# Two small-tile groups padded and moved, so that large SBUF tiles start at multiples of 128 bytes

## The chip, the cores and the metric

The kernel runs as one program on one core of a Trainium2 chip. What counts is the device time of one execution in microseconds (us). Before the change the median of 3 runs is 2946.0 us (2944.36 to 2950.4). "Product" below means one TensorE matrix product: a weight load (LDWEIGHTS) of a stationary operand of 128 x 128 values, and a MATMUL that streams a moving operand of 256 or 512 columns past it.

## What is computed

The reference runs two blocks on one sequence of 512 tokens with 1,024 channels, all in float32.

The first block has two layers. A layer is a SwiGLU feed-forward part of width 2,816 (`x + 0.5 * rms_norm(swiglu(rms_norm(x))))`), a token-mixing part (sliding-window attention with rotary positions, an mLSTM and an RWKV-7 recurrence, joined and projected), a second feed-forward part, and a gated per-layer embedding. The second block is an attention block (global grouped-query attention and a dilated-window mixture) and a feed-forward part with a 3-tap convolution over tokens and a GELU gate.

```python
def first_block(x, ...):
    for l in range(DEPTH):                       # 2 layers
        x = x + 0.5 * rms_norm(swiglu(rms_norm(x, ...), w_ffn1_in[l], w_ffn1_out[l]), ...)
        x = x + rms_norm(token_mixing(rms_norm(x, ...), ...), ...)
        x = x + 0.5 * rms_norm(swiglu(rms_norm(x, ...), w_ffn2_in[l], w_ffn2_out[l]), ...)
        gate = sigmoid(rms_norm(x, ...) @ w_ple_gate[l])
        x = x + rms_norm(gate * (p[l] @ w_ple_proj[l]), ...)
def second_block(x, ...):                        # after it
    x = x + mixed @ w_out                        # two attentions
    x = x + conv_ffn(rms_norm_2(x, norm2_g), w_up, conv_w, conv_b, w_down)
```

## The kernel before

**Precision.** Every large product is done with three products of rounded halves (`mm3`, L284 to L289): an operand is split into a rounded part and a rest (`xh` and `xl`, `wh` and `wl`, the two halves of `ts`, of `gs`, of `wx`), ScalarE making the rounded part (L275, L435) and VectorE the rest (L276, L437). L287 multiplies rounded by rounded, L288 and L289 rounded by rest. The 4-byte values stay in SBUF; TensorE reads both operands from there.

**Stages.** `run` calls, for each layer, `ffn` (L634), `mix` (L758), `ffn` again and `ple`, with `rope_tables` once after the first `ffn`, and at the end `block2`, whose last part is a feed-forward phase called `ffn2`. Within a feed-forward part, the input products go in pairs of 128-channel tiles. The first `FIRST` = 2 pairs are classical products (names `psmm<-...`). The others go through `fast_pair` (L450), which replaces eight products of halves by seven (names `psfast<-...`): for each pair 7 x 4 x 3 = 84 products of 256 moving columns. Of the seven, numbers 0, 1 and 5 stream parts of `xh` and `xl`; 2, 3 and 4 stream the sums `ts`; number 6 streams `xh` and `xl` in the four `ffn` calls and a further pair of `ts` tiles in `ffn2` (`keep=True`). The output products (`ffn_out`, `proj_n8`) have tokens on partitions: `gs` is stationary, and weight tiles `wh` and `wl`, in the last group of four `wx`, stream with 512 columns (names `psone<-...`). `mix` uses `psmm` and `pspn` products for its projections, and small products for its recurrences; `block2` uses `pspn` and `psone` products and small ones for its attentions.

**Order.** The order of the instructions on each engine is the order of the program text; `weave` and `staggered` interleave generators by fixed rates. SyncE's queue starts the weight loads (`raw`, 512 KB each, three buffers), GpSimd's queue the gains.

**Where tiles lie.** Tiles stand in pools, and in each partition a pool's tiles follow one another, each rounded up to 32 bytes. Pools follow one another in the order of `setup`: `const` (with `x`, `ct`, `xh`, `xl`, `mhalf`, and the tables `cos` and `sin` that `rope_tables` adds), `wr` (`raw`), `ws` (`wh`, `wl`), `t4`, `t2` and `sg`, and above them the pools of the running phase: first `sm_...` with the small tiles, then the phase's own, such as `g` (11 tiles), `wx` and `yb` in the same places, and `T0` to `T5` (`ts`, later `gs`). `x` starts at a multiple of 128 bytes. `ct` holds 2,402 values, 9,608 bytes, which take 9,632. So `xh` and `xl` (16,384 bytes each) start 32 bytes past a multiple of 128; `mhalf`, `cos` and `sin` take 320 bytes, and `wr`, `ws` and `t4` start 96 past one. The 28 small tiles of `sg` take 896 bytes, so the tiles of the `ffn` phases start 96 past too. In `ffn2` a tile `cv` of 704 bytes comes first, and `g` and `T0` to `T7` start 32 past.

Of the kernel before, what the change touches and what calls it, by code (L numbers as in the profile page):

```python
# [9 lines left out]
F32 = mybir.dt.float32  # L10
# [9 lines left out]
NT, P = 4, 128  # L20
# [5 lines left out]
# ------------------------------------------------------------------ constants (shapes alone)  # L26


def _const_table():
    """Name -> [128, n] tables that depend on the shapes alone."""  # L30
# [55 lines left out]
# per-channel vectors of a layer, [128, n] columns  # L86
PV_OFF, PV_N = _offsets({k: np.zeros((1, n)) for k, n in (
    ("mu", 8), ("w0", 2), ("a0", 2), ("kk", 2), ("ka", 2), ("rk", 2), ("conv", 16))})
# per-token rows of a layer
# [7 lines left out]
def lay_out(inp):  # L97
    """The inputs in the layouts that the kernel loads: reshapes, transposes, slices and joins."""
# [4 lines left out]
    def chans(v):  # [n*128] -> [128, n]  # L103
        return v.reshape(-1, P).T
# [10 lines left out]
    def t_chunks(w):  # [K, n*128] -> [n, 128, 8, 128]  # L115
        return c(w.reshape(KD, P, -1, P).transpose(2, 1, 0, 3))

    def n_chunks(w):  # [K, n] -> [128, K/128, n]
        return c(w.reshape(-1, P, w.shape[1]).transpose(1, 0, 2))

    def halves(w):  # [K, 1024] -> [2, 128, K/128, 512]
        return c(w.reshape(-1, P, 2, 512).transpose(2, 1, 0, 3))
# [30 lines left out]
def staggered(gens, depth, lag):  # L153
    """The generators one after another, up to depth of them at a time, each lag steps behind the one before."""
    todo, live = list(gens), []
    since = lag
    while todo or live:
        if todo and len(live) < depth and (since >= lag or not live):
            live.append(todo.pop(0))
            since = 0  # L160
        for g in list(live):
            if next(g, live) is live:
                live.remove(g)
        since += 1
        yield


def weave(*streams):
    """Advance the generators together, each by its number of steps in turn (a fraction: now and then)."""
    live = [[g, rate, 0.0] for g, rate in streams]  # L170
    while live:
        for s in list(live):
            s[2] += s[1]
            while s[2] >= 1:
                s[2] -= 1
                if next(s[0], live) is live:
                    live.remove(s)
                    break


# products between the steps of a stream, and rates of the streams woven together
LAG, EARLY, OTHERS, DELTA, SLIDING, MLSTM = 24, 1, 2, 1, 1.3, 1
FIRST = 2  # pairs of tiles by classical products; the rest by fast_pair


class Kernel:
    def __init__(self, tc, io, out):
        self.tc, self.nc, self.io, self.out = tc, tc.nc, io, out
        self.order = list("ABCD")  # pairs of banks, those that are free first first
# [4 lines left out]
    # -------------------------------------------------------------- pools and constants  # L194
    def setup(self, es):
# [10 lines left out]
        self.ct = self.const.tile([P, C_N], F32, name="consts")  # L206

        def early_x(t):
# [5 lines left out]
                     lambda: nc.sync.dma_start(self.ct[:, P:], self.io["consts"][:, P:])]  # L214
# [3 lines left out]
        nc.gpsimd.memset(self.mhalf, -0.5)  # L218

# [14 lines left out]
    def ring(self, **rings):  # L234
        """Name the pairs of banks that bank() takes in turn."""
# [28 lines left out]
    # -------------------------------------------------------------- pieces  # L264
    def rsqrt(self, out, in_, scale, add, tag="rs"):
        """out = (in_ * scale + add) ** -0.5"""
# [6 lines left out]
    def split(self, h, l, src):  # L273
        """h + l = src exactly; each has 12 significant bits."""
# [9 lines left out]
    def mm3(self, out, a, b, start, stop, **kw):  # L284
        """out += a[0+1]^T b[0+1]"""
# [5 lines left out]
    def norm_begin(self):  # L291
        """Begin on the next of the norms; its tokens may come while the phase before still ends."""
# [15 lines left out]
    def norm_token(self):  # L308
        """rms_norm(x) * gain of the next 128 tokens, transposed and split"""
# [23 lines left out]
    def norm_t(self):  # L333
        """The next norm's result, transposed and split: two tiles [128, 8, 512]"""
# [7 lines left out]
    def norm_fast(self):  # L342
        """norm_t, with what fast_parts takes"""
# [29 lines left out]
    def fast_parts(self, pool, ps, keep=False):  # L373
        """What the products of fast_pair take: B[k half][token half] = [[b11, b12], [b21, b22]] gives t1 = b12 - b11,
        t2 = b22 - t1, t3 = b22 - b12 and t4 = b21 - t2"""
# [25 lines left out]
    def ahead(self, jobs):  # L401
        """jobs are (what prepares, what takes that and returns what is left to do); each is prepared before the one
        before it does what is left"""
# [17 lines left out]
    def fast_weights(self, w1, w2):  # L421
        """What fast_pair takes of w1 = [a11 a12] and w2 = [a21 a22], chunks [128, 8, 128]: a11, a12, s2, s1, s3, s4
        and a22, with s1 = a21 + a22, s2 = s1 - a11, s3 = a11 - a21, s4 = a12 - s2, each split"""
# [26 lines left out]
    def fast_pair(self, ws, xb, top, low):  # L450
        """[top; low] = [a11 a12; a21 a22]^T B in seven products of halves (Strassen, Winograd's form); the low half's
        first tokens stay in PSUM."""
# [31 lines left out]
    def proj_t_steps(self, xs, tiles, first=0):  # L484
        """Transposed products: tiles is a list of (chunk [128, 8, 128] in DRAM, what takes the sum).
        The first ones go by token halves, as the later tokens come later."""
# [25 lines left out]
    def proj_n_steps(self, lhs, jobs, ahead=1):  # L512
        """Products with tokens on partitions: lhs(k, t) -> (hi, lo) [128, 128]; the jobs are (w [128, 8, n] in
        DRAM, what takes (token tile, sum), its ring of banks); the pieces of w come some pairs of k ahead."""
# [25 lines left out]
    def proj_n8(self, lhs, w, kn, take, pairs, pool=None, last=4, group=3, ahead=True):  # L540
        """Products with tokens on partitions, up to 1024 columns at once: w [128, kn, n] in DRAM, pairs the
        banks of the tokens, pool(i) two tiles for the pieces of the last group, or None; take(t, sums). With
        ahead the next norm begins before the end."""
# [41 lines left out]
    def post8(self, gain, mul, room):  # L585
        """What takes y [512, 1024]: x += mul * rms_norm(y) * gain; room(t) is a tile [128, 2, 512] for y * gain"""
# [20 lines left out]
    # -------------------------------------------------------------- ffn  # L607
# [62 lines left out]
    # -------------------------------------------------------------- per-layer embedding  # L670
# [38 lines left out]
    # -------------------------------------------------------------- rope tables of the first block  # L709
    def rope_tables(self):  # L710
        self.load_late()
        self.cos = self.const.tile([P, NT, 8], F32, name="cos")
        self.sin = self.const.tile([P, NT, 8], F32, name="sin")
# [3 lines left out]
    def rope_tables_(self):  # L717
        """cos and sin of positions * inv_freq, [128, 4, 8]; the angles are reduced to [-pi, pi] for any
        int32 position: first by multiples of 2 pi 2^11, then of 2 pi, each constant in short parts whose
        products with the counts are exact."""  # L720
# [36 lines left out]
    # -------------------------------------------------------------- token mixing  # L757
    def mix(self, l):  # L758
# [3 lines left out]
        with self.phase(f"mix{l}") as pool:  # L762
            tl = lambda name, shape, dt=F32: pool.tile(list(shape), dt, tag=name, name=name)
            pv = tl("pv", [P, PV_N])
            nc.sync.dma_start(pv, io[f"pv{l}"])
            rows = tl("rows", [P, RW_N])
            nc.gpsimd.dma_start(rows, io[f"rw{l}"][0].partition_broadcast(P))
# [10 lines left out]
            omu = tl("omu", [P, 8])  # L778
            V.tensor_scalar(omu, pv[:, PV_OFF["mu"][0]:PV_OFF["mu"][0] + 8], -1.0, 1.0, ALU.mult, ALU.add)
            hb = tl("hb", [P, 4])  # L780
            V.tensor_scalar(hb, pv[:, PV_OFF["w0"][0]:PV_OFF["w0"][0] + 4], 0.5, None, ALU.mult)
            oka = tl("oka", [P, 2])
# [6 lines left out]
            # ---- rwkv: products, token shift  # L789
# [37 lines left out]
            def prepare():  # L827
# [7 lines left out]
                for i in range(2):  # L835
# [21 lines left out]
                    # kk, normalised by head  # L857
# [34 lines left out]
            # ---- rwkv: blocks of 128 tokens, chunks of 64  # L892
# [4 lines left out]
            def group(t):  # L897
# [9 lines left out]
                # heads of one parity share the rows of the array, and have banks of their own  # L907
# [126 lines left out]
                # group norm, bonus, gate  # L1034
# [24 lines left out]
            # ---- the other products  # L1059
# [35 lines left out]
            def others():  # L1095
# [5 lines left out]
                while len(ab) < 2:  # its tiles are prepare's before  # L1101
                    yield
# [8 lines left out]
            # ---- the three together  # L1111
# [6 lines left out]
            # ---- out  # L1118
# [18 lines left out]
    def sliding(self, pool, qk, va, sinks, out):  # L1137
# [3 lines left out]
        for t in range(NT):  # L1141
            # rope
# [11 lines left out]
            # split, scaled by 1/8 for q, and transposed  # L1154
# [88 lines left out]
    def mlstm(self, pool, X, conv, vo, iff, row, out):  # L1243
# [3 lines left out]
        # gates, tokens on partitions  # L1247
# [7 lines left out]
        # log sigmoid(f) = -log(1 + e), e = exp(-f); log(1 + e) = e * log(w) / (w - 1), w = fl(1 + e)  # L1255
# [8 lines left out]
        # heads on partitions: G = cumsum(log f), a = i - G, M = cummax(a)  # L1264
# [71 lines left out]
    # -------------------------------------------------------------- second block  # L1336
    def block2(self):
# [3 lines left out]
        with self.phase("b2") as pool:  # L1341
# [18 lines left out]
            def head_stat(x, n):  # L1360
                """per-head rms norm of x [128, n, 64]: the scales"""
# [7 lines left out]
            def head_scale(x, r, gi, n):  # L1369
                """per-head rms norm of x [128, n, 64], in place"""  # L1370
# [23 lines left out]
            def head_norms(todo, depth=2):  # L1394
                """per-head norms in place, each after the scales of the next ones: todo is (x [128, n, 64], index of
                the gain, n, tokens for rope or None)"""
# [28 lines left out]
            # products of two 64-vectors a and b in two passes: [ah; al] with [bh; bl] and with [bl; bh]  # L1425
            def split_q(q, n):
                """Four heads, scaled by 1/8: [qh | ql]"""
# [9 lines left out]
            def split_k(src, dst):  # L1437
                """[kh | kl | kh]"""
# [24 lines left out]
            def prepare(kind, h):  # L1463
                """What head h of the first (kind 0) or second attention needs"""
# [92 lines left out]
            # norms of the outputs, transposed  # L1557
# [19 lines left out]
        with self.phase("ffn2") as pool:  # L1577
            cv = pool.tile([P, 4, 44], F32, name="cv")
            nc.sync.dma_start(cv, io["cv2"].rearrange("p (j m) -> p j m", j=4))
# [81 lines left out]
```

## Time and profile before

| what | before |
|---|---|
| median of 3 runs | 2946.0 us (2944.36 to 2950.4) |
| span of the profiled execution | 2960.7 us |
| TensorE matmuls | busy 2898.4 us (98%), 19,000 |
| TensorE weight loads | busy 2538.6 us (86%) |
| VectorE | busy 1953.1 us (66%) |
| ScalarE | busy 1425.6 us (48%) |
| GpSimd | busy 140.3 us (5%) |
| DMA | 250.91 MB, mean 85 GB/s |

The profile is of one execution, whose own time is its span; it stands 14.7 us (0.5%) above the median of the runs. "Busy" of a matmul runs from its start to a modelled end, and consecutive matmuls overlap, so the time that a product costs is read from start to start and not from its mean duration. The rows are quoted in the section ahead of the prediction.

### The profile page before, as it was taken

What the parts mean: (1) busy time and instruction counts of PE and PEld (TensorE: products, weight loads), DVE (VectorE), ACT (ScalarE), POOL (GpSimd) and SP (SyncE); (2) the same over time, 40 slices, a digit from 0 to 9 for tenths busy, and PEclk for the clock granted to TensorE, in tenths of its full rate; (3) what the DMA queues carried; (4) which work ended last, traced back from release to release, by engine and by line L of the source; (5) the groups of instructions that cost most, each with busy time, mean ns of one, the idle gap of its engine ahead of it and who ended that gap; (6) DMA issues with size and microseconds to landing.
All of it is one profiled execution on the core that took longest, in us unless ns stands there. A gap on an engine that the chain in (4) does not pass through costs nothing. (4 is left out here: it accounts for less than half of the span.)

```text
span 2960.7 us, 47335 instructions
## 1 busy us (share of the span) xinstructions
PE 2898.4 (98%) x19000; PEld 2538.6 (86%) x19000; DVE 1953.1 (66%) x3464; ACT 1425.6 (48%) x2784; POOL 140.3 (5%) x169
## 2 busy tenths in 40 slices
PE   7999999999999999999999999999999999999999
PEld 7998887877999878999887877799987877789987
DVE  7884555756888357886345655688635766688853
ACT  5663343343666245555334233456534456566641
POOL 0000000101000000000000000100000220000000
PEclk9999999999999999999999988999999999999999
DMA  4333322002233332333412000233343210313332
GB/s 152 108 122 103 97 81 65 8 8 65 93 115 115 100 103 90 109 107 116 130 56 79 15 8 29 75 107 111 114 128 90 93 43 1 93 62 104 100 101 91
DMA packets 74156, 250.91 MB, mean 85 GB/s; under 512 B 8112, under 2 KB 10416, under 8 KB 73680
## 3 DMA queue, kind: packets, MB, share of 16 engines
q1 hardware_dynamic: 70992, 236.99, 25.2%
q0 software_dynamic: 2944, 10.90, 1.1%
q8 instruction: 149, 2.44, 0.3%
q14 instruction: 71, 0.58, 0.1%
HBM read 245.76 MB, written 2.10 MB: 84 GB/s over the span
## 5 line engine op out<-in xcount | busy, mean ns | idle before, releaser
L276 DVE TENSOR_TENSOR wl<-raw,wh 128x1024 fp32r<-128x1024 f32 (+2 forms) x218 | 259.2, 1193 | 410.1 <-ACT wh L275 408.5
L275 ACT CAST wh<-raw 128x1024 fp32r<-128x1024 f32 (+2 forms) x218 | 223.4, 1026 | 469.9 <-PE psone L289 316.9
L287 PE MATMUL psfast<-xh,wh 128*128 128x256 f32 x1448 | 401.9, 278 | 0.0
L289 PE MATMUL psfast<-xh,wl 128*128 128x256 f32 x1448 | 400.7, 277 | 0.0
L288 PE MATMUL psfast<-xl,wh 128*128 128x256 f32 x1448 | 400.6, 277 | 0.0
L287 PE MATMUL psfast<-ts,wh 128*128 128x256 f32 x1184 | 333.1, 282 | 0.0
L289 PE MATMUL psfast<-ts,wl 128*128 128x256 f32 x1184 | 333.0, 281 | 0.0
L288 PE MATMUL psfast<-ts,wh 128*128 128x256 f32 x1184 | 332.5, 281 | 0.0
L288 PE MATMUL psone<-wl,gs 128*128 128x512 f32 x720 | 284.2, 395 | 0.0
L289 PE MATMUL psone<-wh,gs 128*128 128x512 f32 x720 | 284.1, 395 | 0.0
L287 PE MATMUL psone<-wh,gs 128*128 128x512 f32 x720 | 282.3, 395 | 0.0
L287 PEld LDWEIGHTS psfast<-xh,wh 128*128 128x128 f32 x1448 | 272.0, 188 | 1.3
L288 PEld LDWEIGHTS psfast<-xl,wh 128*128 128x128 f32 x1448 | 272.1, 188 | 0.5
L289 PEld LDWEIGHTS psfast<-xh,wl 128*128 128x128 f32 x1448 | 272.0, 188 | 0.0
L435 ACT CAST wh<-raw 128x512 fp32r<-128x512 f32 x282 | 174.7, 621 | 157.8 <-PE psfast L288 154.2
L287 PEld LDWEIGHTS psfast<-ts,wh 128*128 128x128 f32 x1184 | 222.7, 188 | 0.7 <-ACT top L465 0.7
L289 PEld LDWEIGHTS psfast<-ts,wl 128*128 128x128 f32 x1184 | 222.9, 188 | 0.0
L288 PEld LDWEIGHTS psfast<-ts,wh 128*128 128x128 f32 x1184 | 222.8, 188 | 0.0
L437 DVE TENSOR_TENSOR wl<-raw,wh 128x1024 fp32r<-128x1024 f32 (+1 forms) x188 | 179.1, 953 | 64.9 <-ACT wh L435 64.5
L287 PE MATMUL psmm<-xh,wh 128*128 128x256 f32 (+1 forms) x616 | 206.8, 338 | 0.1
L288 PE MATMUL psmm<-xl,wh 128*128 128x256 f32 (+1 forms) x616 | 205.8, 335 | 0.0
L289 PE MATMUL psmm<-xh,wl 128*128 128x256 f32 (+1 forms) x616 | 204.3, 333 | 0.0
(545 smaller groups left out, 6494.1 us busy)
## 6 DMA issues: line engine op xcount, KB each, us to landing
raw<-f1i SPq DMA_DIRECT2D x88, 512.0 KB, 3.5
raw<-f2i SPq DMA_DIRECT2D x88, 512.0 KB, 3.5
raw<-f1o SPq DMA_DIRECT2D x44, 512.0 KB, 3.7
raw<-f2o SPq DMA_DIRECT2D x44, 512.0 KB, 3.9
raw<-w2u SPq DMA_DIRECT2D x44, 512.0 KB, 3.5
raw<-w2d SPq DMA_DIRECT2D x22, 512.0 KB, 3.9
gain<-gains POOLq DMA_DIRECT2D x19, 512.0 KB, 4.0
raw<-wr SPq DMA_DIRECT2D x16, 512.0 KB, 3.6
```

The lines of the kernel that those rows point to most:

```text
L275: self.rounded = self.nc.scalar.copy(h, src)
L276: self.nc.vector.tensor_sub(l, src, h.bitcast(F32))
L287: mm(out, a[0], b[0], start=start, stop=False, **kw)
L288: mm(out, a[0], b[1], start=False, stop=False, **kw)
L289: mm(out, a[1], b[0], start=False, stop=stop, **kw)
L435: nc.scalar.copy(h[:, i], src[:, i])
L437: sub(l, src, h.bitcast(F32))
```

## The change

Small tiles get more room, and small tiles that stood alone share one:

- `ct` is allocated with 2,432 columns in place of 2,402 (9,728 bytes, 76 x 128).
- `cos` and `sin`, 128 bytes each and allocated in `rope_tables`, become two parts of one tile `tables` of 80 columns (320 bytes) in `setup`; with `mhalf` (64 bytes) that is 384 bytes, 3 x 128.
- In `mix`, `pv` has 64 columns in place of 34, `rows` 800 in place of 784; `omu`, `hb` and `oka`, three tiles before, become parts of one tile `vecs` of 32 columns.
- In `ffn2`, `cv` is [128, 4, 48] in place of [128, 4, 44], and its load fills the first 44 of each 48.

No operation of a compute engine is added or removed, and no loop changes. The loads of `ct`, `pv`, `rows` and `cv` bring the same bytes; that of `cv` writes four runs of 176 bytes in each partition where it wrote one of 704. The comments and doc strings of the file are removed too.

The positions that follow, as bytes past a multiple of 256 (and of 128 in brackets):

| tiles | before | after |
|---|---|---|
| `xh`, `xl` | 32 (32) | 128 (0) |
| `raw`, `wh`, `wl`, tiles of `t4` | 96 (96) | 0 (0) |
| `g`, `wx`, `ts`, `gs` in the four `ffn` | 224 (96) | 128 (0) |
| `g`, `wx`, `ts`, `gs` in `ffn2` | 160 (32) | 128 (0) |
| `x`, `ct` and its identity | 128 (0) | 128 (0) |

Within all these tiles the parts that TensorE reads begin at further multiples of 512 bytes, so a product's operands have the position of their tile. Of the large tiles only `vo1` to `vo3` in `mix` stay 32, 64 and 96 bytes past.

```diff
+LINE = 32
 FIRST = 2
@@ setup
-        self.ct = self.const.tile([P, C_N], F32, name="consts")
+        whole = lambda n: -(-n // LINE) * LINE
+        self.ct = self.const.tile([P, whole(C_N)], F32, name="consts")
...
-                     lambda: nc.sync.dma_start(self.ct[:, P:], self.io["consts"][:, P:])]
+                     lambda: nc.sync.dma_start(self.ct[:, P:C_N], self.io["consts"][:, P:])]
...
         nc.gpsimd.memset(self.mhalf, -0.5)
+        tables = self.const.tile([P, 3 * LINE - 16], F32, name="tables")
+        self.cos, self.sin = [tables[:, 32 * i:32 * i + 32].rearrange("p (t j) -> p t j", t=NT) for i in range(2)]
@@ rope_tables
-        self.cos = self.const.tile([P, NT, 8], F32, name="cos")
-        self.sin = self.const.tile([P, NT, 8], F32, name="sin")
@@ mix
-            pv = tl("pv", [P, PV_N])
-            nc.sync.dma_start(pv, io[f"pv{l}"])
-            rows = tl("rows", [P, RW_N])
-            nc.gpsimd.dma_start(rows, io[f"rw{l}"][0].partition_broadcast(P))
+            pv = tl("pv", [P, 2 * LINE])
+            nc.sync.dma_start(pv[:, 0:PV_N], io[f"pv{l}"])
+            rows = tl("rows", [P, 25 * LINE])
+            nc.gpsimd.dma_start(rows[:, 0:RW_N], io[f"rw{l}"][0].partition_broadcast(P))
...
-            omu = tl("omu", [P, 8])
+            vecs = tl("vecs", [P, LINE])
+            omu, hb, oka = vecs[:, 0:8], vecs[:, 8:12], vecs[:, 16:18]
             V.tensor_scalar(omu, pv[:, PV_OFF["mu"][0]:PV_OFF["mu"][0] + 8], -1.0, 1.0, ALU.mult, ALU.add)
-            hb = tl("hb", [P, 4])
             V.tensor_scalar(hb, pv[:, PV_OFF["w0"][0]:PV_OFF["w0"][0] + 4], 0.5, None, ALU.mult)
-            oka = tl("oka", [P, 2])
@@ block2, ffn2
-            cv = pool.tile([P, 4, 44], F32, name="cv")
-            nc.sync.dma_start(cv, io["cv2"].rearrange("p (j m) -> p j m", j=4))
+            cv = pool.tile([P, 4, 48], F32, name="cv")
+            nc.sync.dma_start(cv[:, :, 0:44], io["cv2"].rearrange("p (j m) -> p j m", j=4))
```

## Rows read from the trace of the kernel before

**Rows 1.** The page, part 1: busy time, share of the span, instructions of each engine.

```profile
PE 2898.4 (98%) x19000; PEld 2538.6 (86%) x19000; DVE 1953.1 (66%) x3464; ACT 1425.6 (48%) x2784; POOL 140.3 (5%) x169
```

**Rows 2.** The chain that ended last, shares of the span by engine.

```profile
PE 44%; DVE 2%; POOL 1%; ACT 1%; issue 0%; DMA 0%; POOLq 0%; ACTq 0%; DVEq 0%
```

**Rows 3.** Matmuls by form: line, out<-in, shapes, count | busy us, mean ns.

```profile
L287 PE MATMUL psfast<-xh,wh 128*128 128x256 f32 x1448 | 401.9, 278 | 0.0
L287 PE MATMUL psfast<-ts,wh 128*128 128x256 f32 x1184 | 333.1, 282 | 0.0
L287 PE MATMUL psone<-wh,gs 128*128 128x512 f32 x720 | 282.3, 395 | 0.0
L287 PE MATMUL psmm<-xh,wh 128*128 128x512 f32 x280 | 111.4, 398 | 0.0
L287 PE MATMUL psmm<-xh,wh 128*128 128x256 f32 x336 | 95.4, 289 | 0.1
L287 PE MATMUL pspn<-wh,xh 128*128 128x512 f32 x224 | 90.6, 404 | 0.0
L287 PE MATMUL psone<-wx,gs 128*128 128x512 f32 x160 | 63.0, 394 | 0.0
```

**Rows 4.** Matmuls in order of time, first ffn: start us, duration us, instruction.

```profile
110.92 0.28 PE L287 MATMUL psfast<-xh,wh 128*128 128x256 f32 x1
...
116.37 0.28 PE L287 MATMUL psfast<-ts,wh 128*128 128x256 f32 x1
...
120.64 0.28 PE L287 MATMUL psfast<-xh,wh 128*128 128x256 f32 x1
```

**Rows 5.** Matmuls in order of time, output products of the first ffn.

```profile
240.33 0.39 PE L287 MATMUL psone<-wh,gs 128*128 128x512 f32 x1
...
340.76 0.40 PE L287 MATMUL psone<-wx,gs 128*128 128x512 f32 x1
...
357.13 0.60 PE L321 MATMUL pstr<-consts,xn 128*128 128x128 f32 x4
```

**Rows 6.** Matmuls in order of time, ffn2.

```profile
2697.29 0.28 PE L287 MATMUL psfast<-ts,wh 128*128 128x256 f32 x1
...
2698.70 0.28 PE L287 MATMUL psfast<-xh,wh 128*128 128x256 f32 x1
...
2833.47 0.39 PE L287 MATMUL psone<-wh,gs 128*128 128x512 f32 x1
...
2934.27 0.39 PE L287 MATMUL psone<-wx,gs 128*128 128x512 f32 x1
...
2955.60 0.39 PE L288 MATMUL psone<-wx,gs 128*128 128x512 f32 x1
```

**Rows 7.** Matmuls in order of time, projections of mix and of block2.

```profile
385.99 0.39 PE L287 MATMUL psmm<-xh,wh 128*128 128x512 f32 x1
...
410.49 0.61 PE L812 MATMUL psD<-consts,x 128*128 128x128 f32 x4
...
2344.37 0.40 PE L287 MATMUL pspn<-wh,xh 128*128 128x512 f32 x1
...
2410.30 0.93 PE L1457 MATMUL psO<-consts,ks 128*128 128x128 f32 x7
```

**Rows 8.** Matmuls in order of time, a run of narrow products in mix.

```profile
611.38 1.45 PE L1308 MATMUL psD<-vo,es 128*128 128x65 f32 x12
612.67 0.50 PE L1227 MATMUL psC<-va,PT 128*128 128x64 f32 x3
```

**Rows 9.** VectorE by form, same size at two positions: mean ns after the busy time.

```profile
L276 DVE TENSOR_TENSOR xl<-pstr,xh 128x512 fp32r<-128x512 f32 x88 | 57.1, 683 | 7.8 <-ACT xh L275 7.4
L605 DVE TENSOR_TENSOR x<-psone,x 128x512 f32<-128x512 f32 x16 | 11.0, 691 | 33.6 <-PE psone L289 33.6
```

**Rows 10.** Busy time by stretch, first ffn: PE, PEld, DVE, ACT, POOL, granted clock, DMA.

```profile
100.00:200.00 100.00, 100.00 (x866) 100.00 (x865) 84.57 (x133) 60.23 (x125) 0.00 (x0) 1.00 0.31 111
```

**Rows 11.** DMA issues: count, KB each, median us from issue to landing.

```profile
cv<-cv SPq DMA_DIRECT2D x1, 88.0 KB, 1.8
```

## The prediction

> **What bounds the kernel now.** First the busy time of each engine: TensorE's matmuls fill 98% of the span and its weight loads, which run beside them, 86%; VectorE has 66%, ScalarE 48% [rows 1]. Then the chain that ended last: of the engines TensorE holds 44% of the span on it, no other more than 2%, and DMA 0% [rows 2]. So the kernel is a row of matrix products, and a time that each of some 19,000 products loses or gains is lost or gained at the end. Third the matmuls by form: seven forms of the rounded product carry the counts, and each stands three times in the program, once for each of L287, L288 and L289 [rows 3]. The idle time in those rows is 0.0 or 0.1 us: TensorE doesn't wait for data, so what can change is the rate at which it takes products.
>
> The mean durations of [rows 3] overlap and don't give that rate. It is read from start to start over a stretch of equal products. In the first ffn the 48 products of 256 columns that stream `xh` or `xl` take (116.37 - 110.92)/48 = 113.5 ns each; the 36 that stream sums take (120.64 - 116.37)/36 = 118.6 [rows 4]. The two have the same columns, weights and engine; what differs is the tile that streams. At 512 columns: (340.76 - 240.33)/432 = 232.5 ns for `wh,gs`, and (357.13 - 340.76)/72 = 227.4 for `wx,gs` [rows 5]. In ffn2 the sums take (2698.70 - 2697.29)/12 = 117.5, `wh,gs` (2934.27 - 2833.47)/432 = 233.3, `wx,gs` (2955.60 - 2934.27)/94 = 226.9 [rows 6]. The projections: `xh` in `mix` (410.49 - 385.99)/105 = 233.3, and with `xh` stationary (2410.30 - 2344.37)/288 = 228.9 [rows 7]. [...]
>
> [...]
>
> **What the change can reach.** It moves bytes in SBUF and no operation. VectorE shows no sensitivity to it: 512 elements take 683 ns into `xl`, 32 bytes past a multiple of 128, and 691 into `x`, on one [rows 9]. So engines off the path stay as they are, and the change is worth what it does to TensorE's intervals.
>
> What position does to them is shown by no pair of rows alone, since no product of before has both large operands on a multiple of 128. [...] Distance: what counts is how far the moving operand stands from the next stationary one, past a multiple of 256. Moving minus stationary is, in bytes: `xh` 192 (113.5 ns), sums in ffn 128 (118.6), in ffn2 64 (117.5); at 512 columns `wh,gs` 128 (232.5), `wx,gs` 0 (227.4), ffn2 192 (233.3) and 0 (226.9), `mix` 192 (233.3), `xh` stationary 64 (228.9). Equal distances have equal times at 512 columns, which speaks for distance. But 192 is the best at 256 columns and the worst at 512, so distance alone is no law; and `xh` and ffn2's sums, both 32 past a multiple of 128, differ by 4 ns, so neither is the moving position.
>
> [...]
>
> **The sum.** I take that with both operands on a multiple the products of each shape come to the lowest interval that this shape shows, 113.5 at 256 columns and 227.0 at 512. Counts are three times those of [rows 3], and two forms are split by the text: of 3,552 sums' products 80 pairs x 36 = 2,880 are in the four ffn and 14 x 48 = 672 in ffn2; of 2,160 `wh,gs` 1,728 and 432.
> - sums in ffn 2,880 x 5.1 ns = 14.7 us; in ffn2 672 x 4.0 = 2.7
> - `wh,gs` in ffn 1,728 x 5.5 = 9.5; in ffn2 432 x 6.3 = 2.7
> - `psmm` of 512 columns 840 x 6.3 = 5.3; `pspn` 672 x 1.9 = 1.3
>
> That is 36.2 us. Besides, no row has both operands on a multiple, so a step below the lowest is open. Its ends: at 256 columns 107.5 (the narrow run) and 118.6 (the sums), at 512 columns 213.3 (columns alone) and 233.3. I take 113.0 and 224.5, close to the nearest rows, `xh` and `wx,gs`. Over 4,344 + 3,552 + 1,008 = 8,904 products of 256 columns 0.5 ns is 4.5 us, and over 2,160 + 480 + 840 + 672 = 4,152 of 512 columns 2.5 ns is 10.4 us. Together -51 us. With every product at the lower ends the sum is -71 - 76 = -147 us; with every one at the upper ends +28 + 7 = +35 us. The profiled execution's 2960.7 us is its span, 14.7 us over the median of the runs and 0.5% of it; a sum of intervals carries over, so 2946.0 - 51 = 2895 us.
>
> What could eat it: VectorE is busy 84.57 of 100 us in the densest stage, beside TensorE's 100 [rows 10], so TensorE can be 15% faster before VectorE is late, and 2% is asked. The small edits I take as 0. `tables` and `vecs` hold what stood alone, with the same writers in the same order; a wait between parts of one tile could cost one VectorE operation, some 0.7 us, in each of two layers, or nothing. The load of `cv` lands in 1.8 us [rows 11] and will have 512 runs of 176 bytes in place of 128; with four times the time it lands in 7 us, 5 later. It is issued as ffn2 begins, and its first reader follows the first pair's products, so those hide it; without that cover the cost is 5 us, 0.2%. Nothing on SP's queue behind it is wanted sooner than the three `raw` buffers allow.
>
> **The rivals.** [...]
>
> *Distance decides, and the change makes it worse.* After it nearly every large product has its operands 128 bytes apart past a multiple of 256 (0 against 128), the distance at which the sums of ffn stand now and are the slowest; only `wx,gs` keeps 0. Then `xh` goes from 113.5 to 118.6, 4,344 x 5.1 = 22.2 us; `psmm` of 256 columns 1,008 x 5.1 = 5.1; ffn2's sums 672 x 1.1 = 0.7; `pspn` 672 x (232.5 - 228.9) = 2.4; `psmm` of 512 and ffn2's `wh,gs` gain 840 x 0.8 and 432 x 0.8, 1.0: +29.4 us, 2975 us, 1.0% slower. [...] For it: 128 is the slowest distance at 256 columns, and equal distances agree to 0.5 ns at 512. Against it: every row at distance 128 is of operands 96 bytes past a multiple of 128 too, so the two can't be told apart there.
>
> *Nothing.* The intervals follow from what else differs, such as the order of parts in a tile or the banks of PSUM, and position doesn't enter: 2946 us, within 6. For it: no row isolates position. Against it: `wh,gs` and `wx,gs`, with the same order, differ by 5 ns [rows 5], and again in ffn2 by 6 [rows 6].
>
> **How the numbers follow.** The forecast has 0.40, with a range of its own of 2870 to 2925; the whole sixteenth 0.22; nothing 0.12; distance 0.26. About 0.2%, 6 us, is what a measurement of this kernel can tell from no change. So faster has 0.40 + 0.22 = 0.62, the same 0.12, slower 0.26. The range goes from 2835, 25 us under the whole sixteenth and 36 over the lower ends of the sum (2946 - 147 = 2799), to 2975, the price of distance: outside lie the upper part of that last case and the tail of the second, under 2 in 10.
>
> **What would show it.** Right: in the first ffn `xh` and the sums both at 113 ns from start to start, `wh,gs` and `wx,gs` alike at 224 to 227, the projections too; VectorE's 683 ns unchanged; the first products of ffn2 no later after the load of `cv`. [...] Distance: `xh` at 118.6 while `wx,gs` stays at 227 and `wh,gs` at 232. Nothing: the old intervals in their places. I would be wrong above all if the sums stay where they are, since they and `xh` carry most of the products.

## The result

The changed kernel takes 2974.6 us (median of 6 runs, 2970.8 to 2987.2), the kernel before 2947.0 in runs beside them: slower by 27.6 us, ratio 1.0095 with a 95% interval of 1.0067 to 1.0123. The forecast was 2895 us and faster. The rival that the distance between operands decides had 2975 us and a chance of 0.26.

The first part of the page and the chain by engine, after the change:

```profile
PE 2906.2 (98%) x19000; PEld 2552.0 (86%) x19000; DVE 1958.7 (66%) x3464; ACT 1425.8 (48%) x2784; POOL 138.1 (5%) x169
...
PE 44%; DVE 3%; POOL 1%; ACT 1%; issue 0%; DMA 0%; POOLq 0%; ACTq 0%; DVEq 0%
```

The bound is the same as in [rows 1, 2]: TensorE is still at 98%, with no new wait. Its products come more slowly. The same three products of the first ffn as in [rows 4], in order of time:

```profile
112.42 0.28 PE L291 MATMUL psfast<-xh,wh 128*128 128x256 f32 x1
...
118.12 0.28 PE L291 MATMUL psfast<-ts,wh 128*128 128x256 f32 x1
...
122.39 0.28 PE L291 MATMUL psfast<-xh,wh 128*128 128x256 f32 x1
```

`xh` now takes (118.12 - 112.42)/48 = 118.7 ns where it took 113.5; the sums (122.39 - 118.12)/36 = 118.6, as before. The products of [rows 5] and, from 2705.41 on, those of [rows 6]:

```profile
245.00 0.39 PE L291 MATMUL psone<-wh,gs 128*128 128x512 f32 x1
...
345.41 0.39 PE L291 MATMUL psone<-wx,gs 128*128 128x512 f32 x1
...
361.75 0.82 PE L325 MATMUL pstr<-consts,xn 128*128 128x128 f32 x6
...
2705.41 0.28 PE L291 MATMUL psfast<-ts,wh 128*128 128x256 f32 x1
...
2706.83 0.28 PE L291 MATMUL psfast<-xh,wh 128*128 128x256 f32 x1
...
2842.13 0.39 PE L291 MATMUL psone<-wh,gs 128*128 128x512 f32 x1
...
2942.51 0.39 PE L291 MATMUL psone<-wx,gs 128*128 128x512 f32 x1
```

`wh,gs` stays at (345.41 - 245.00)/432 = 232.4 ns and `wx,gs` at (361.75 - 345.41)/72 = 226.9; in ffn2 the sums have gone from 117.5 to (2706.83 - 2705.41)/12 = 118.3 and `wh,gs` from 233.3 to (2942.51 - 2842.13)/432 = 232.4. The projection with `xh` stationary, [rows 7], has gone from 228.9 to 232.4:

```profile
2351.20 0.40 PE L291 MATMUL pspn<-wh,xh 128*128 128x512 f32 x1
...
2418.12 0.93 PE L1458 MATMUL psO<-consts,ks 128*128 128x128 f32 x7
```

That is (2418.12 - 2351.20)/288. VectorE did not move. The two VectorE forms of [rows 9] after the change:

```profile
L280 DVE TENSOR_TENSOR xl<-pstr,xh 128x512 fp32r<-128x512 f32 x88 | 57.4, 684 | 8.4 <-ACT xh L279 8.1
L609 DVE TENSOR_TENSOR x<-psone,x 128x512 f32<-128x512 f32 x16 | 11.1, 691 | 33.5 <-PE psone L293 33.5
```

And the load of [rows 11]:

```profile
cv<-cv SPq DMA_DIRECT2D x1, 88.0 KB, 2.5
```

VectorE has 684 and 691 ns where it had 683 and 691, and `cv` lands in 2.5 us where it took 1.8.

The spans of the two profiled executions, 2960.7 and 2969.0 us, differ by 8.3 us only, since that of before is from a run of 2962.7 us in which the granted clock fell in the second `mix`. The window from 1700 to 1800 us before the change (PE, PEld, DVE, ACT, POOL busy, granted clock, DMA):

```profile
1700.00:1800.00 100.00, 99.41 (x661) 80.33 (x661) 48.38 (x163) 33.90 (x108) 4.21 (x4) 0.77 0.02 6
```

The same window after it:

```profile
1700.00:1800.00 100.00, 98.44 (x773) 80.56 (x773) 60.19 (x197) 39.59 (x124) 7.83 (x7) 0.96 0.02 7
```

The kernel before was granted 0.77 of the full clock there, where the changed one had 0.96, and issued 661 products instead of 773. So medians, and the intervals of products at a clock of 1.00, are what can be compared.

### The profile page after: what moved, and what is told of

Same layout as the page of the kernel before. It is cut to its first block, busy times and chain, and to the rows that moved or that the text cites. A ratio compares the mean times of both kernels' runs of the same rounds, so it can differ in the third digit from the quotient of the medians.

```text
span 2969.0 us, 47335 instructions
## 1 busy us (share of the span) xinstructions
PE 2906.2 (98%) x19000; PEld 2552.0 (86%) x19000; DVE 1958.7 (66%) x3464; ACT 1425.8 (48%) x2784; POOL 138.1 (5%) x169
## 5 line engine op out<-in xcount | busy, mean ns | idle before, releaser
L291 PE MATMUL psfast<-xh,wh 128*128 128x256 f32 x1448 | 408.5, 282 | 0.0
L293 PE MATMUL psfast<-xh,wl 128*128 128x256 f32 x1448 | 407.6, 282 | 0.0
L292 PE MATMUL psfast<-xl,wh 128*128 128x256 f32 x1448 | 407.6, 281 | 0.0
```

What stands on the lines that cost most here:

```text
L291: mm(out, a[0], b[0], start=start, stop=False, **kw)
L292: mm(out, a[0], b[1], start=False, stop=False, **kw)
L293: mm(out, a[1], b[0], start=False, stop=stop, **kw)
```

## The experiments

Two theories stood after the result. **Distance:** a product's interval is set by its columns and by the moving operand's position less the stationary one's, past a multiple of 256. **Own position:** a stream that itself begins on a multiple of 128 is the slow one. In the changed kernel `xh` has both. The table holds the mean interval from start to start, in ns, over the products of a form, without the few intervals more than some 15% longer than the rest, and the distance in bytes in brackets; the last row is what the intervals of all products with 256 columns or more add up to against before.

| products | count | before | after | ct alone | tables alone | near 192 | zero | split |
|---|---|---|---|---|---|---|---|---|
| `xh`, 256, fast | 4,344 | 113.9 (192) | 118.7 (128) | 113.8 (192) | 118.6 (128) | 114.3 (192) | 113.8 (192) | 113.4 (192) |
| sums, ffn | 2,880 | 118.8 (128) | 118.7 (128) | 118.8 (128) | 118.7 (128) | 114.4 (192) | 119.5 (0) | 113.3 (192) |
| sums, ffn2 | 672 | 117.8 (64) | 119.1 (128) | 117.8 (64) | 117.6 (64) | 113.6 (192) | 119.4 (0) | 114.2 (192) |
| `xh`, 256, `psmm` | 1,008 | 115.2 (192) | 119.0 (128) | 116.1 (192) | 118.9 (128) | 115.5 (192) | 115.9 (192) | 114.9 (192) |
| `wh,gs`, ffn | 1,728 | 232.4 (128) | 232.4 (128) | 233.1 (128) | 232.4 (128) | 229.0 (64) | 227.0 (0) | 226.9 (0) |
| `wh,gs`, ffn2 | 432 | 233.3 (192) | 232.4 (128) | 233.3 (192) | 233.4 (192) | 232.6 (64) | 226.8 (0) | 226.8 (0) |
| `wx,gs`, ffn | 384 | 227.6 (0) | 227.5 (0) | 227.6 (0) | 227.6 (0) | 227.5 (0) | 227.3 (0) | 227.3 (0) |
| `pspn`, 512 | 672 | 229.5 (64) | 232.3 (128) | 229.5 (64) | 232.3 (128) | 229.5 (64) | 229.4 (64) | 229.4 (64) |
| sum, us | | 0 | +26.6 | +1.7 | +25.7 | -20.0 | -9.8 | -34.0 |

**One part of the change alone: ct.**

```diff
-        self.ct = self.const.tile([P, C_N], F32, name="consts")
+        self.ct = self.const.tile([P, 2432], F32, name="consts")
...
-                     lambda: nc.sync.dma_start(self.ct[:, P:], self.io["consts"][:, P:])]
+                     lambda: nc.sync.dma_start(self.ct[:, P:C_N], self.io["consts"][:, P:])]
```

> Only ct is widened, so xh, xl and every tile behind them move by 96 bytes: xh stands on a multiple of 128, the weights 64 past one, and every distance between a moving and a stationary tile is that of the kernel before. Distance decides: no change, 2947 us, xh at 113.5 to 114 ns from start to start, sums at 118.6. The own position decides (a stream that begins on a multiple of 128 is the slow one): xh at 118.7 as in the changed kernel, 4,344 + 1,008 products x 4.8 ns, about +26 us, 2973 us.

Measured: 2948.6 us, before beside it 2946.6, ratio 1.0011 (0.9997 to 1.0024). No change that can be told from none. The trace, as [rows 4]:

```profile
110.01 0.28 PE L287 MATMUL psfast<-xh,wh 128*128 128x256 f32 x1
...
115.46 0.28 PE L287 MATMUL psfast<-ts,wh 128*128 128x256 f32 x1
```

`xh` begins on a multiple of 128 and takes (115.46 - 110.01)/48 = 113.5 ns. Own position falls.

**The other part alone: tables.**

```diff
+        tables = self.const.tile([P, 80], F32, name="tables")
+        self.cos, self.sin = [tables[:, 32 * i:32 * i + 32].rearrange("p (t j) -> p t j", t=NT) for i in range(2)]
...
-        self.cos = self.const.tile([P, NT, 8], F32, name="cos")
-        self.sin = self.const.tile([P, NT, 8], F32, name="sin")
```

> Only cos and sin become one tile of 320 bytes, so the weights and all that lies behind them move by 64 bytes; xh stays 32 past a multiple of 128, no large tile stands on a multiple of 128, and the distance of xh to the weights becomes 128 past a multiple of 256. Distance decides: xh at 118.7 ns, the whole loss, about +27 us, 2974 us. The own position decides: xh keeps 113.5 to 114 ns, 2947 us.

Measured: 2970.8 us against 2946.6, ratio 1.0081 (1.0066 to 1.0096). Here no large tile of the feed-forward parts is on a multiple of 128, and the loss is nearly all there:

```profile
111.92 0.28 PE L289 MATMUL psfast<-xh,wh 128*128 128x256 f32 x1
...
117.62 0.28 PE L289 MATMUL psfast<-ts,wh 128*128 128x256 f32 x1
```

(117.62 - 111.92)/48 = 118.7 ns. So 64 bytes more between `xh` and the weights made the change slow.

**That part undone in the changed kernel.**

```diff
-        tables = self.const.tile([P, 3 * LINE - 16], F32, name="tables")
...
+        self.cos = self.const.tile([P, NT, 8], F32, name="cos")
+        self.sin = self.const.tile([P, NT, 8], F32, name="sin")
```

> The changed kernel with cos and sin as two tiles again, so that the weights and all behind them lie 64 bytes lower: xh stays on a multiple of 128 and is 192 from the weights again; the padding of ct, the merged vecs and the new cv stay. Distance decides: xh at 113.9 ns, sums at 118.7 in ffn and in ffn2 (672 x 1.2 = +0.8 us), wh,gs in ffn2 at 232.4 (-0.4): 2947 us, the time of before. Rival, the small edits of mix and ffn2 (vecs, pv, rows, cv) have a price of their own, the 4 us that lie between the changed kernel and the one with tables alone: about 2951 us.

Measured: 2946.9 us against 2948.1, ratio 0.9991 (0.9962 to 1.0020). `ct`, `vecs`, `pv`, `rows` and `cv` cost nothing that can be measured, and `xh`, on a multiple of 128 and 192 from the weights, has its old interval, (114.47 - 109.02)/48 = 113.5 ns:

```profile
109.02 0.28 PE L289 MATMUL psfast<-xh,wh 128*128 128x256 f32 x1
...
114.47 0.28 PE L289 MATMUL psfast<-ts,wh 128*128 128x256 f32 x1
```

**TensorE alone.** The two operands are slices of two tiles; 48 products, a cell, for each pair of positions. The program ran once.

```diff
+            for i in range(count):
...
+                nc.tensor.matmul(p[:, 0:n], sta[:, s0:s0 + 128], mov[:, m0:m0 + n], start=i == 0, stop=i == count - 1)
```

> None of the kernel's work: only products of TensorE alone, 48 for each cell, with 256 or 512 moving columns, at sixteen distances between moving and stationary operand (0 to 480 bytes past a multiple of 512), at four stationary positions for four of the distances, and at distances 4 to 24 bytes off 192; and cells whose stationary operand alternates between two positions. Distance decides: at 256 columns 113.5 to 114 ns at 192, 118.7 at 128, 117.7 at 64; at 512 columns 227 at 0, 229 at 64, 232 at 128, 233 at 192; the same at each stationary position, and the same at d and d + 256. The own position decides: equal distances differ between stationary positions. [...]

Measured, ns from start to start after the first five of a cell:

```
distance              0     32     64     96    128    160    192    224
256 columns       120.0  117.7  117.8  119.9  118.6  118.7  117.8  118.3
512 columns       226.7  233.3  228.9  233.5  233.4  234.2  233.4  233.2
256 to 480 more: the same eight values, to 0.1 ns
stationary 32, 96, 128, 288 past, at distances 0, 64, 128, 192:
256 columns       119.8 to 120.0, 117.8, 118.7 to 118.8, and 113.4 to 113.5 (once 117.8)
512 columns       226.9 to 227.2, 228.8, 232.4, 233.3 to 233.4
```

With no other engine at work, distance past a multiple of 256 and the number of columns give the intervals of the kernel, nearly whatever the position. Two things were missed. At 256 columns distance 192 has two levels, 117.8 at positions 0 and 32 and 113.4 to 113.5 at the others. At 512 columns distance 128 has 233.4 at position 0 and 232.4 elsewhere. Distances 4, 8, 16 and 24 bytes above 192 gave 122.3, 122.2, 119.3 and 121.1 at 256 columns. The cells whose stationary operand alternates between two positions gave 113.6 to 119.9, some of them not the mean of their two distances (64 and 0 in turn 116.7, alone 117.8 and 120.0); they settle nothing. Three groups of 192 products at 256 columns, each with its stationary position in its name (start, length, count):

```profile
125.99 22.93 PE L223 MATMUL p256w32m<-mov,sta 128*128 128x256 f32 x192
148.76 22.75 PE L223 MATMUL p256w96m<-mov,sta 128*128 128x256 f32 x192
171.34 22.74 PE L223 MATMUL p256w128m<-mov,sta 128*128 128x256 f32 x192
```

(148.76 - 125.99)/192 = 118.6 ns is the mean of the four distances at position 32, with 117.8 at 192; (171.34 - 148.76)/192 = 117.6 that at 96, with 113.5.

**Distance 192 for the sums.** The kernel before, with 64 bytes ahead of the phases' tiles, and `cv` as in the change:

```diff
+        self.sg.tile([P, 16], F32, tag="pad", name="pad", bufs=1)
...
-            cv = pool.tile([P, 4, 44], F32, name="cv")
-            nc.sync.dma_start(cv, io["cv2"].rearrange("p (j m) -> p j m", j=4))
+            cv = pool.tile([P, 4, 48], F32, name="cv")
+            nc.sync.dma_start(cv[:, :, 0:44], io["cv2"].rearrange("p (j m) -> p j m", j=4))
```

> The kernel before with 64 bytes of padding ahead of the phases' tiles and 64 more in cv: no large tile stands on a multiple of 128, but sums stand 192 from the weights as xh does, wh stands 64 from gs, wx 0 from xh in ple. Distance decides, and 192 gives the sums what it gives xh: sums at 113.5 to 114 ns (2,880 x 5.0 + 672 x 4 = 17 us), wh,gs at 229 (1,728 x 3.4 + 432 x 4.3 = 8 us), wx,xh 227 (288 x 6 = 2 us): -27 us, 2920 us. Rival, the second level that the probe showed at 192: sums at 117.8, and only 2.4 us of the 17: about 2934 us. Rival, the lower interval belongs to xh and its place in the order: sums stay at 118.6, about 2936 us.

Measured: 2926.4 us against 2947.1, ratio 0.9934 (0.9922 to 0.9947).

```profile
115.00 0.28 PE L288 MATMUL psfast<-ts,wh 128*128 128x256 f32 x1
...
119.08 0.28 PE L288 MATMUL psfast<-xh,wh 128*128 128x256 f32 x1
...
236.26 0.39 PE L288 MATMUL psone<-wh,gs 128*128 128x512 f32 x1
...
335.30 0.39 PE L288 MATMUL psone<-wx,gs 128*128 128x512 f32 x1
```

The sums come at (119.08 - 115.00)/36 = 113.3 ns, `wh,gs` at (335.30 - 236.26)/432 = 229.3: the lower interval never belonged to `xh`. Some 6 us of the 27 are missing. Most of them lie with products that took a second, higher level at an unchanged distance. In the third of the four `ffn` calls sums and `xh` kept to it throughout:

```profile
1242.45 0.28 PE L288 MATMUL psfast<-ts,wh 128*128 128x256 f32 x1
...
1246.69 0.28 PE L288 MATMUL psfast<-xh,wh 128*128 128x256 f32 x1
...
1252.35 0.28 PE L288 MATMUL psfast<-ts,wh 128*128 128x256 f32 x1
```

(1246.69 - 1242.45)/36 = 117.8 ns for the sums and (1252.35 - 1246.69)/48 = 117.9 for `xh`, where the other three calls have 113.3; the table's 114.4 and 114.3 are this mixture and stand for some 2 us each. So the rival of the second level holds for a quarter of the sums. In ffn2 `wh,gs` begins near 229 and goes over to 233.3 after some 80 products:

```profile
2834.68 0.40 PE L288 MATMUL psone<-wh,gs 128*128 128x512 f32 x1
...
2901.89 0.40 PE L288 MATMUL psone<-wx,gs 128*128 128x512 f32 x1
```

(2901.89 - 2834.68)/288 = 233.4; its mean is 232.6 instead of 229 (1.6 us).

**Distance 0 for sums and gs.** The same with 128 bytes (`[P, 32]` in place of `[P, 16]`).

> As the run with 192, but with 128 bytes of padding: sums, gs and wx at distance 0 from the weights, a distance that no stream of 256 columns had in the kernel before or in the changed one. By the probe's table: sums at 119.9 (2,880 x 1.3 + 672 x 2.1 = +5 us), wh,gs at 227 (1,728 x 5.4 + 432 x 6.3 = -12 us), wx,xh at 229 (288 x 4 = -1 us): -8 us, 2939 us. Rival, the closer the two operands the better at each shape: sums near 113 as well, -31 us, 2916 us.

Measured: 2939.0 us against 2947.1, ratio 0.9954 (0.9930 to 0.9979). The two shapes part as the cells say: the sums get slower, 119.5 by the table, and `wh,gs` faster, 227.0; below (120.66 - 116.36)/36 = 119.4 and (338.87 - 240.64)/432 = 227.4. Nearest is not best.

```profile
116.36 0.28 PE L288 MATMUL psfast<-ts,wh 128*128 128x256 f32 x1
...
120.66 0.29 PE L288 MATMUL psfast<-xh,wh 128*128 128x256 f32 x1
...
240.64 0.39 PE L288 MATMUL psone<-wh,gs 128*128 128x512 f32 x1
...
338.87 0.39 PE L288 MATMUL psone<-wx,gs 128*128 128x512 f32 x1
```

**Each shape at its own best.** The same 128 bytes, and the sums 192 bytes up in wider tiles; `gs`, in the same tiles later, begins at their start:

```diff
-        ts = [[pool.tile([P, 4, 256], F32R, tag=f"T{2 * i + j}", name="ts") for j in range(2)] for i in range(3)]
+        up = lambda i: pool.tile([P, 1088], F32R, tag=f"T{i}", name="ts")[:, 48:1072].rearrange("p (k n) -> p k n", k=4)
+        ts = [[up(2 * i + j) for j in range(2)] for i in range(3)]
...
+        two = pool.tile([P, 1088], F32R, tag=f"T{(2, 3, 0, 1, 4, 5)[n % 6]}", name="gs")
+        return two[:, 0:S], two[:, S:2 * S]
```

> As the run with distance 0, with the tiles T0 to T7 256 bytes wider, the sums 192 bytes up in them and gs at their start: each of the two has the distance that is lowest for its shape, 192 for sums and 0 for gs. Distance decides: sums 113.5 to 114 (-17 us), wh,gs 227 (-12 us), wx,xh 229 (-1 us): -30 us, 2916 us. Rival, the second level at 192: sums at 117.8, about 2930 us.

Measured: 2918.2 us against 2947.1, ratio 0.9910 (0.9895 to 0.9926), faster than both kernels: 29 us under before, and 56 under the changed one's median, which was not run beside it.

```profile
114.00 0.28 PE L288 MATMUL psfast<-ts,wh 128*128 128x256 f32 x1
...
118.08 0.28 PE L288 MATMUL psfast<-xh,wh 128*128 128x256 f32 x1
...
235.26 0.39 PE L288 MATMUL psone<-wh,gs 128*128 128x512 f32 x1
...
333.43 0.39 PE L288 MATMUL psone<-wx,gs 128*128 128x512 f32 x1
```

(118.08 - 114.00)/36 = 113.3 and (333.43 - 235.26)/432 = 227.2 ns; all four `ffn` calls are at the lower level. The table's -34.0 us is of the profiled execution, which took 2913.2 us, the shortest of its four.

**How the load bears on it.** A second program of TensorE alone, run once:

> None of the kernel's work: products of TensorE alone, 48 for each cell. First with stationary operands of 128, 64 and 32 columns. [...] Then distances in steps of 4 bytes at one stationary position; distance 192 at sixteen stationary positions and after different cells, to see which of 113.5 and 117.8 comes and whether what went before decides it; and a stationary operand that changes after every second product, which tells whether the interval goes by the operand in use or by the next one.

Stationary operands of 128, 64 and 32 columns; each row is 192 products, 48 at each of the distances 0, 64, 128, 192:

```profile
44.56 22.74 PE L212 MATMUL c128n256d<-mov,sta 128*128 128x256 f32 x192
67.14 44.41 PE L212 MATMUL c128n512d<-mov,sta 128*128 128x512 f32 x192
111.40 22.51 PE L212 MATMUL c64n256d<-mov,sta 128*64 128x256 f32 x192
133.75 44.34 PE L212 MATMUL c64n512d<-mov,sta 128*64 128x512 f32 x192
177.92 21.96 PE L212 MATMUL c32n256d<-mov,sta 128*32 128x256 f32 x192
199.72 44.60 PE L212 MATMUL c32n512d<-mov,sta 128*32 128x512 f32 x192
```

At 256 columns a load of 128 columns gives 120.0, 117.8, 118.7 and 113.5 ns at the four distances, one of 64 gives 113.3, 116.7, 116.6 and 118.8, and one of 32 gives 113.3 to 113.5 at all four. So at 256 columns the spread over the four distances is 6.5 ns with a load of 128, 5.5 with one of 64 and 0.2 with one of 32, and at 512 it shrinks too, from 6.7 to 4.3 and 1.0 ns. That would fit a stream and a load that are in each other's way; no run shows that they are. But the load of 32 does not go below the lowest interval of a load of 128: (199.72 - 177.92)/192 = 113.5 ns is what a load of 128 has at distance 192, and at 512 columns the load of 32 has 230.8 to 231.7, above the 226.7 that a load of 128 has at distance 0.

In steps of 4 bytes, the lowest at 256 columns is 113.3 ns, at 16 and 192 (113.8 at 112), the highest 123.0 at 4; at 512 columns the lowest is 227.2, at 0, and the highest 240.0, at 20 and others. No position measured brings a product of 256 columns under 113.3 ns, or one of 512 under 226.7.

Distance 192 at sixteen stationary positions alternated from cell to cell:

```profile
1328.30 5.63 PE L212 MATMUL s0d<-mov,sta 128*128 128x256 f32 x48
1333.77 5.82 PE L212 MATMUL s32d<-mov,sta 128*128 128x256 f32 x48
1339.42 5.63 PE L212 MATMUL s64d<-mov,sta 128*128 128x256 f32 x48
1344.89 5.82 PE L212 MATMUL s96d<-mov,sta 128*128 128x256 f32 x48
```

The intervals are 113.3 and 117.8 in turn: (1333.77 - 1328.30)/48 is 114.0 and (1339.42 - 1333.77)/48 is 117.7, with the change of cell in it. Position 96 had 113.5 in the first probe and 113.4 in the scan by 4 bytes; here, and after cells of 512 columns, it has 117.8. So neither distance nor position decides which of the two comes; what differs is what went before, and a row of products can stay in either. Distance 128 has two as well: 118.7 in the first cells, 120.0 in the six cells that come after distance 192 at 117.8. What chooses is open. Inconclusive: the stationary operand that changes after every second product gave mixtures (231.8 to 232.5 at all four positions), so whether the operand in use or the next one counts was not told apart.

## Why the prediction was wrong

**The bound was right.** TensorE's intervals set the time (they add up to +26.6 us, and the medians differ by 27.6), other engines and DMA don't: after the change VectorE has 3% of the chain and DMA 0%. The small edits at nothing (ratio 0.9991 in the changed kernel with the tables part undone), the untouched 683 ns (now 684) and the cover of VectorE (busy 83.49 us of the window from 100 to 200 us, beside TensorE's 100) held.

**The step that failed** is the first of the sum: "with both operands on a multiple the products of each shape come to the lowest interval that this shape shows". Position by itself did nothing (ct alone: `xh` on a multiple, 113.5 ns as before), and both operands on a multiple did no more: in the changed kernel the sums have both and come at 118.6. Each of its terms went with its distance: the sums in ffn, 14.7 us forecast, kept 128 and gave 0.3; `wh,gs` in ffn, 9.5 us forecast, kept 128 and gave nothing; `xh`, from which nothing but the half nanosecond was expected, went from 192 to 128 and lost 20.8 us; `pspn`, 1.3 us forecast, lost 1.9. In ffn2 the sums, 2.7 us forecast, lost 0.9, and `wh,gs`, 2.7 forecast, gave 0.4; `psmm` of 512 columns, 5.3 forecast, gave 0.5 (233.3 to 232.7 ns). The further step below the lowest rows, 14.9 us, has no ground: no position measured gets below 113.3 and 226.7 ns. Of its lower ends, no run shows the 213.3 ns at 512 columns; the 107.5 is the interval of the products of 65 columns in [rows 8], (612.67 - 611.38)/12, and no product of 256 columns came to it. The whole sixteenth, with its chance of 0.22, is a saving on every product, below those intervals, that no run shows; the lower end of the range, 2835 us, stands on it. That the range, 2835 to 2975 us, still holds the time is owed to the rival, whose price is its upper end.

**What led to it** was the sentence that distance is no law because 192 is the best at 256 columns and the worst at 512. That rules out one law for both shapes, not a law for each. Sorted by columns and distance together, [rows 4 to 7] hold no contradiction; sorted by position they do, as the prediction itself said of `xh` and ffn2's sums, both 32 past.

**The rival was right in its rule and nearly in size.** In these runs columns and distance set the interval, up to the two levels; whether the distance counts to the next stationary operand, as it said, or to the one in use is not shown. It had +29.4 us; the intervals add up to +26.6 and the medians differ by 27.6. `xh` was put at 22.2 and is 20.8; `psmm` of 256 columns at 5.1 and is 3.8, since it came at 115.2 before and not at 113.5. The size is partly luck: `xh` ran before at the lower level of distance 192, but for the last part of ffn2, where the trace has 117.7. Had it all run at 117.8, the same step to 118.7 would by estimate have cost 4,344 x 0.9 = 4 us. Two forms that it left out cancel: 576 `psone` products that stream `wh` past `xh` lost 1.5 us (230.1 to 232.7 ns) and 288 that stream `wx` past it won 1.2 (232.4 to 228.3), most of them now at distance 0. The whole sixteenth fell with the lowest intervals of the probes, 113.3 and 226.7 ns, "nothing" with tables alone, ratio 1.0081.

A finer alignment does not decide either. In the scan in steps of 4 bytes, at 512 columns, streams that start 4 bytes above a multiple of 16 take 233.3 to 240.0 ns, but those that start 12 above take 229.5 to 233.3, less on average than the multiples of 16 themselves, which take 227.2 to 236.6.

## What to carry to other kernels

When TensorE streams from SBUF while it loads weights from SBUF, ask how far the two operands stand from each other and not whether they are aligned (`xh` 64 bytes further from the weights cost 0.8%, tables alone; `xh` on a multiple of 128 at its old distance nothing that can be told, ct alone); measure a table of intervals by columns, width of the load and distance once, with a probe of some tens of products a cell, and then place each tile by the shape in which it is read. Do not average over levels: a mean between two table values can be a stretch at one and a stretch at the other (114.4 ns in near 192, from 113.3 and 117.8), so split it by time. A small tile allocated ahead of a pool moves all that lies behind it, so an edit that seems idle cost 0.8% here (tables alone) or gave 0.7% (near 192). In reading rows, sort them by two variables before a variable is thrown out for failing alone.

## What was not expected of the hardware

In the first probe the distance counts past a multiple of 256 bytes: 0 and 256, 32 and 288, and so on agree to 0.1 ns. In the two probes all positions measured with a load of 128 lie between 113.3 and 123.0 ns at 256 columns and between 226.7 and 240.0 at 512. Products of one form at one distance ran at either of two lasting levels and, in ffn2 of near 192, changed between them in mid-row: at 256 columns 113.3 and 117.8 ns at 192 (near 192, second probe) and 118.7 and 120.0 at 128 (second probe); at 512 columns 228.9 (first probe) and 233.3 (near 192) at 64 and, in ct alone, 233.3 in the first three `ffn` calls and 232.4 in the fourth at 128. What chooses the level is open.
